# A hybrid decoder layer on one core: every PSUM tensor cut to 512 columns

## The chip, the core and the metric

The kernel runs on one core of one Trainium2 chip. The metric is the device time of one execution in microseconds; a kernel is timed in several runs and the median is compared. Matrix products run on TensorE (PE in the profile, its weight loads PEld), element-wise work on VectorE (DVE) and ScalarE (ACT). GpSimd (POOL) and SyncE (SP) issue the transfers. Products land in PSUM, which VectorE and ScalarE then read.

## What is computed

The layer normalises `x` (1024 tokens by 1024 channels), modulates it by a conditioning vector, projects it by one wide matrix, runs two gated linear recurrences in parallel, merges their projections and adds the result to `x`. Cut to what matters here:

```python
h = rms_norm(x, norm_w) * (1 + scale) + shift
proj = h @ w_in
hq, hf, hi, hz, gq, gk, gv, gz, ga, mg = split(proj)
y_h = hgrn2_branch(hq, hf, hi, hz, ...)   # 8 heads, 128 keys x 128 values each
y_g = gla_branch(gq, gk, gv, gz, ga, ...) # 4 heads, 128 keys x 256 values each
# both: S_t = diag(a_t) S_{t-1} + k_t v_t^T,  o_t = S_t^T q_t, per head
merged = sigmoid(mg0) * (y_h @ w_branch0) + sigmoid(mg1) * (y_g @ w_branch1)
out = rms_norm(x + gate * (merged @ w_out), final_norm_w)
```

## The kernel before, in words

Products are taken as float32r in three parts (high times high, high times low, low times high), each matmul 128 x 128 weights by 512 columns. The program goes through these stages.

- **First group** (`product`, L386): six feature blocks `f` of the projection, for the first and then for the second half of the tokens. Six accumulators of 512 columns are open at once: four are the halves of two 1024-column tiles `pd` (`accs`, L380 and the lines around it), two are the halves of the scoring tile `sc_ps`. `qk_out` reads each on VectorE (L362, L364) and sends it away.
- **V stages** (`Vstage`, `Vjob`, L1879): the values `gv`, and later `hi`, by a seven-product scheme (`PRODUCTS`), each product in two jobs `kk`. A stage has four banks `i` of 512 columns, again the halves of two `pd` tiles. After the second job of a product `Vstage.after` reads bank `i` (L1762, L1764 on ScalarE; L1786, L1790 on VectorE; for product 3 ScalarE writes a seed back, L1782). A job goes through `i` = 0, 1, 2, 3, six matmuls each.
- **Feature jobs** (`Feat`, `mm_feat`, L594): one head's gate, query or key feature for all 1024 tokens into one `pd` tile, both halves in turn; then one reader takes all 1024 columns: `silu_done` (L949 ScalarE, L950 VectorE), `gla_k_done` (L1016), `hf_done` (L1079, L1080 ScalarE).
- **Heads** (`attention`): side work that is woven between the matmuls of the jobs. VectorE builds `xb` (L645 to L648), TensorE makes the first level's scores in `sc_ps` (L652), VectorE reads them (L659 and the three predicated copies L664 to L666), TensorE makes the second level (L683) in the same tile, and so on.
- **Last stages** (L1330) **and the output product** (L1507): banks of 512 columns are lent by `Banks`: two halves of `sc_ps`, two `pm` tiles, four halves of two `pd` tiles.

PSUM holds eight banks of 512 float32 columns: `ps_d` two tiles of two banks, `sc_ps` one of two banks, `ps_m` two of one bank.

Up to the end of the first half of the first group the order on TensorE, ScalarE and VectorE is the order of the code. After it a scheduler sets the order on each engine from a priority and its own estimate of when operands are free, and it places the semaphore waits. It keeps track of a tile as a whole: a write to a tile is ordered after earlier reads of that tile, whichever columns they took. Each engine then runs its instructions strictly in that order. Slots in SBUF are given out in rotation, so a load can also wait for the last reader of its slot.

Of the kernel before, what the change touches and what calls it, by code (L numbers as in the profile page):

```python
# [16 lines left out]
P = 128  # L17
D = 1024
T = 1024
# [70 lines left out]
def hybrid_trunk_kernel(  # L90
# [20 lines left out]
    def dtile():  # L111
        cnt[0] += 1
        return ps_d.tile([P, T], F32, tag="d", name=f"pd{cnt[0]}")

# [3 lines left out]

    sc_ps = ps_s.tile([P, T], F32, name="sc_ps")

# [108 lines left out]
    def keep_busy(n):  # L229
        for _ in range(n):  # L230
            nc.tensor.matmul(sc_ps[:, 512:640], ones, ident, start=True, stop=True)

# [354 lines left out]
    def mm_feat(wt, rhs, ps, w=P):  # L587
        hi, lo = wt
        for k in range(KT):
            n = 0  # L590
            r_hi, r_lo = rhs(k)
            for a, b in ((hi, r_hi), (hi, r_lo), (lo, r_hi)):
                for th in range(2):
                    nc.tensor.matmul(ps[0:w, th * 512:(th + 1) * 512], a[:, k, 0:w],  # L594
                                     b[:, th * 512:(th + 1) * 512],
                                     start=(k == 0 and n == 0), stop=(k == KT - 1 and n == 2))
                n += 1
            yield
# [27 lines left out]
    def attention(q, k, f, v, V, post, early, lead=3):  # L626
# [23 lines left out]
        for b in range(32):  # L650
            ch, j = b // 4, b % 4
            nc.tensor.matmul(sc_ps[32 * j:32 * j + 32, ch * P:ch * P + 80], k[:, b * 32:b * 32 + 32], xb[:, b, :],  # L652
                             start=True, stop=True)
# [10 lines left out]
        cpr(bv[:, :, :, 1:4], bc(mk[:, :, :, 0:5:2], [NCH, 8, 3]), px[:, :, :, 0:5:2])  # L664
        cpr(bv[:, :, :, 2:4], bc(mk[:, :, :, 1:6:4], [NCH, 8, 2]), px[:, :, :, 1:6:4])
        cpr(bv[:, :, :, 3], bc(mk[:, :, :, 3], [NCH, 8]), px[:, :, :, 3])  # L666
        TT(k4[:, :, :, 0:3], k4[:, :, :, 0:3], f4[:, :, :, 1:4], M)
# [13 lines left out]
        for b in range(32):  # L681
            ch, j = b // 4, b % 4
            nc.tensor.matmul(sc_ps[32 * j:32 * j + 32, ch * 48:ch * 48 + 48], k[:, b * 32:b * 32 + 32],  # L683
                             xf[:, b * 48:b * 48 + 48], start=True, stop=True)
# [32 lines left out]
        keep(16)  # L717
        px = sc_ps[:, 0:384].rearrange("p (g s n) -> p g s n", s=6, n=4)
        bv = blk.rearrange("p c t -> p (c t)").rearrange("p (g r n) -> p g r n", r=4, n=4)
# [19 lines left out]
        for b in range(32):  # L739
            ch, j = b // 4, b % 4  # L740
            nc.tensor.matmul(sc_ps[32 * j:32 * j + 16, 512 + ch * 16:512 + ch * 16 + 16],
                             k16[:, b * 16:b * 16 + 16], q16[:, b * 16:b * 16 + 16], start=True, stop=True)
        for ch in range(NCH):
            for hf in range(2):
                i = 2 * ch + hf
                p0, c0 = 64 * hf + 32 * (ch % 2), ch // 2 * 32
                nc.tensor.matmul(sc_ps[p0:p0 + 32, c0:c0 + 32], k32[:, i * 32:i * 32 + 32],
                                 q32[:, i * 32:i * 32 + 32], start=True, stop=True)
        for ch in range(NCH):
            s0 = ch * P  # L750
            p0, c0 = ch % 2 * 64, 640 + ch // 2 * 64
            nc.tensor.matmul(sc_ps[p0:p0 + 64, c0:c0 + 64], k[:, s0:s0 + 64],
                             q[:, s0 + 64:s0 + 128], start=True, stop=True)
        grow(64)
        cur = off[1]
        cpr(blk[:, :, 16:32], bc(masks[16], [NCH, 16]),
            sc_ps[:, 512:640].rearrange("p (c t) -> p c t", c=NCH))
        for hf in range(2):
            for odd in range(2):
                p0 = 64 * hf + 32 * odd  # L760
                nc.scalar.copy(scT[64 * hf:64 * hf + 32, odd::2, 64 * hf + 32:64 * hf + 64],
                               sc_ps[p0:p0 + 32, 0:128].rearrange("p (c t) -> p c t", t=32))
        for odd in range(2):
            nc.scalar.copy(scT[0:64, odd::2, 64:128],
                           sc_ps[64 * odd:64 * odd + 64, 640:896].rearrange("p (c t) -> p c t", t=64))
        scoring.discard(me)
# [179 lines left out]
    def silu_done(store, key):  # L946
        def f(ps):
            s = S.get([T])
            nc.scalar.activation(s, ps, AF.Sigmoid)  # L949
            nc.vector.tensor_mul(s, s, ps)  # L950
            store[key] = s
        return f
# [60 lines left out]
    def gla_k_done(h):  # L1013
        def f(ps):
            t = S.get([T])
            nc.vector.tensor_copy(t, ps)  # L1016
# [59 lines left out]
    def hf_done(h):  # L1076
        def fn(ps):
            f, k = S.get([T]), S.get([T])
            nc.scalar.activation(f, ps, AF.Sigmoid)  # L1079
            nc.scalar.activation(k, ps, AF.Sigmoid, scale=-1.0)  # L1080
# [568 lines left out]
    def scores_done():  # L1649
        while scoring or head_no[0] < 12:  # L1650
            stream.weave(1)
        R.lend([sc_ps[:, 0:512], sc_ps[:, 512:1024]])

# [93 lines left out]
    class Vstage:  # L1747
# [226 lines left out]
```

## Time and profile before

| | |
|---|---|
| median of 3 runs | 1201.26 us (1200.64 to 1201.57) |
| the profiled execution: its own time | 1201.55 us |
| its span, first to last instruction | 1199.8 us |
| first group | 20 to 116 us |
| V stage of `gv` | 112 to 199 us |
| feature jobs and GLA heads, V stage of `hi` within | 199 to 423 us |
| feature jobs and HGRN heads | 423 to 797 us |
| last stages and output product | 797 to 1200 us |

A row of the timeline gives the start, the duration, engine, line, operation, `out<-in`, the size, the count of merged instructions and, in brackets, the time that the engine was idle before it and who ended that idle time. Matmuls are pipelined: one of 512 columns is shown 0.39 us long while the next starts 0.23 us after it, so a shown idle time understates a gap between starts by some 0.16 us.

### The profile page before, as it was taken

To read this page: it belongs to the slowest core of one execution; us is meant where nothing else is said; L and a number is where in the kernel's file an instruction comes from. 1 tells how busy PE (TensorE), PEld (TensorE's weight loads), DVE (VectorE), ACT (ScalarE), POOL (GpSimd) and SP (SyncE) were. 2 spreads that over 40 slices of the span, in tenths; PEclk is the share of its full clock that TensorE was granted. 3 is DMA by queue.
4 is the path that set the end of the run, shared out by engine and by line. 5 is a ranking of instruction groups with operands and counts; after the bars stand their busy time and mean duration, and the time that the engine had idled before them with its cause. 6 is when DMAs were issued, how large, how long until landed. Compare 5 with 4: busy or idle time off the path is not lost.

```text
span 1199.8 us, 20303 instructions
## 1 busy us (share of the span) xinstructions
PE 1170.1 (98%) x8137; PEld 951.0 (79%) x8137; DVE 846.3 (71%) x1270; ACT 584.9 (49%) x860; POOL 124.3 (10%) x257
## 2 busy tenths in 40 slices
PE   7999999999999999999999999999999999999997
PEld 6776777888878688888888878778888888878886
DVE  4745667657664955887897798695553866988994
ACT  5674462673455445334433435456643644444554
POOL 4111111000110211111111010001120000000000
PEclk9999999999999999999999999999999999999999
DMA  9745445155474855665565454255688846335523
GB/s 324 262 173 201 150 161 176 52 178 175 167 273 141 296 195 161 209 210 160 173 197 178 130 203 124 78 169 179 225 312 284 285 152 210 125 108 173 171 99 134
DMA packets 150641, 221.24 MB, mean 184 GB/s; under 512 B 8971, under 2 KB 107329, under 8 KB 150546
## 3 DMA queue, kind: packets, MB, share of 16 engines
q1 hardware_dynamic: 132114, 158.37, 42.4%
q0 software_dynamic: 18384, 61.56, 13.3%
q8 instruction: 64, 1.05, 0.4%
q14 instruction: 31, 0.25, 0.1%
q10 hardware_dynamic: 48, 0.01, 0.0%
HBM read 154.37 MB, written 65.54 MB: 183 GB/s over the span
## 4 chain that ended last, share of the span: by engine, by line
PE 65%; issue 20%; DVE 6%; ACT 4%; DMA 3%; POOL 2%; SPq 0%; POOLq 0%; DVEq 0%; ACTq 0%
PE pd L594 16%; PE pd L1330 11%; PE pd L1879 9%; PE sc_ps L1330 6%; PE pm L1330 6%; PE pd L1507 3%; PE pd L386 2%; PE sc_ps L1507 2%; PE pm L1507 1%; PE pm L798 1%; POOL ws L1182 1%; DVE b L212 1%; PE pm L817 1%; DMA b<-in_ada_w_dram 1%; PE sc_ps L386 1%
## 5 line engine op out<-in xcount | busy, mean ns | idle before, releaser
L594 PE MATMUL pd<-b,b 128*128 128x512 f32 x1632 | 393.8, 396 | 0.2 <-ACT b L1762 0.2
L594 PEld LDWEIGHTS pd<-b,b 128*128 128x128 f32 x1632 | 303.0, 189 | 65.8 <-issue 0.7
L1330 PE MATMUL pd<-b,b 128*128 128x512 f32 x720 | 173.2, 392 | 0.6 <-DVE b L1422 0.4
L1879 PE MATMUL pd<-b,b 128*128 128x512 f32 x672 | 162.7, 396 | 7.1 <-DVE b L1790 3.4
L1330 PEld LDWEIGHTS pd<-b,b 128*128 128x128 f32 x720 | 133.9, 188 | 31.2 <-DVE b L1422 0.9
L1879 PEld LDWEIGHTS pd<-b,b 128*128 128x128 f32 x672 | 123.4, 188 | 40.7 <-ACT b L1762 4.0
L212 DVE TENSOR_TENSOR b<-b,b 128x1024 fp32r<-128x1024 f32 x78 | 94.2, 1222 | 48.4 <-ACT b L211 48.1
L1273 DVE TENSOR_TENSOR b<-b,b 128x1024 fp32r<-128x1024 f32 x56 | 68.2, 1221 | 69.2 <-ACT b L1272 53.0
L1272 ACT CAST b<-b 128x1024 fp32r<-128x1024 f32 x56 | 58.4, 1050 | 65.0 <-PE pm L1330 18.1
L211 ACT CAST b<-b 128x1024 fp32r<-128x1024 f32 x78 | 79.8, 1047 | 6.4 <-PE pd L1879 3.0
L1330 PE MATMUL sc_ps<-b,b 128*128 128x512 f32 x324 | 78.7, 391 | 0.4 <-ACT b L1302 0.4
L1330 PE MATMUL pm<-b,b 128*128 128x512 f32 x300 | 72.1, 389 | 0.0
L1330 PEld LDWEIGHTS sc_ps<-b,b 128*128 128x128 f32 x324 | 60.4, 188 | 13.9 <-ACT b L1302 1.1
L1249 ACT CAST b<-b 128x1024 fp32r<-128x1024 f32 x48 | 49.7, 1050 | 43.9 <-PE pd L1330 15.9
L1250 DVE TENSOR_TENSOR b<-b,b 128x1024 fp32r<-128x1024 f32 x48 | 57.7, 1219 | 18.4 <-ACT b L1249 12.2
L1330 PEld LDWEIGHTS pm<-b,b 128*128 128x128 f32 x300 | 56.3, 188 | 11.7
L203 DVE TENSOR_TENSOR b<-b,b 128x1024 fp32r<-128x1024 f32 (+1 forms) x36 | 35.1, 983 | 29.5 <-ACT b L202 29.4
L386 PE MATMUL pd<-b,b 128*128 128x512 f32 x192 | 52.3, 405 | 2.8 <-DVE b L362 1.9
L1182 POOL DMA_DIRECT2D ws<-b x64 | 34.9, 546 | 193.6 <-DVE b L1174 107.4
L703 ACT COPY xb<-b 128x512 f32<-128x512 f32 x48 | 29.7, 621 | 50.8 <-PE sc_ps L683 23.8
L817 PE MATMUL pm<-scT,b 128*128 128x128 f32 x256 | 46.9, 275 | 0.0
L386 PEld LDWEIGHTS pd<-b,b 128*128 128x128 f32 x192 | 34.4, 188 | 15.4 <-DVE b L362 2.9
(317 smaller groups left out, 1699.6 us busy)
## 6 DMA issues: line engine op xcount, KB each, us to landing
b<-in_w_in_dram SPq DMA_DIRECT2D x72, 512.0 KB, 4.3
ws<-b POOLq DMA_DIRECT2D x64, 256.0 KB, 3.9
b<-ws SPq DMA_DIRECT2D x32, 512.0 KB, 4.4
b<-in_x_dram SPq DMA_DIRECT2D x16, 512.0 KB, 4.4
b<-in_ada_w_dram SPq DMA_DIRECT2D x32, 256.0 KB, 6.5
v<-b POOLq DMA_DIRECT2D x32, 256.0 KB, 3.7
b<-v SPq DMA_DIRECT2D x16, 512.0 KB, 5.2
b<-fx SPq DMA_DIRECT2D x16, 512.0 KB, 4.5
```

The lines of the kernel that those rows point to most:

```text
L211: held(nc.scalar.copy(hi, src))
L212: nc.vector.tensor_sub(lo, src, hi.bitcast(F32))
L386: nc.tensor.matmul(accs[f], wg(a, d, f), b[d][:, half * 512:half * 512 + 512], start=(d == 0 and n == 0), stop=(d == KT - 1 and n == 2))
L594: nc.tensor.matmul(ps[0:w, th * 512:(th + 1) * 512], a[:, k, 0:w], b[:, th * 512:(th + 1) * 512], start=(k == 0 and n == 0), stop=(k == KT ...
L817: nc.tensor.matmul(o, vch(ch)[:, vh * P:(vh + 1) * P], scT[:, ch, :], start=True, stop=(ch == 0))
L1249: nc.scalar.copy(hi, src)
L1250: nc.vector.tensor_sub(lo, src, hi.bitcast(F32))
L1272: nc.scalar.copy(hi, t)
L1273: nc.vector.tensor_sub(lo, t, hi.bitcast(F32))
L1330: nc.tensor.matmul(o, a[:, sl], c, start=(p in (1, 5) and kt == 0 and n == 0), stop=(kt == 3 and n == 2), skip_group_check=True)
L1507: nc.tensor.matmul(o, a, b, start=(p in (1, 5) and kt == 0 and n == 0), stop=(kt == 3 and n == 2), skip_group_check=True)
L1879: nc.tensor.matmul(st.bank[i], x_, w_, start=(p in (1, 5) and kk == 0 and a == 0 and n == 0), stop=(kk == 1 and a == 1 and n == 2), skip_g ...
```

## The change

`ps_d` now has four tiles of one bank each instead of two of two. `dtile` returns a list of two of them, and the scoring tile is a list of two. All users take the halves from these lists. The order of the code is kept; where one instruction read 1024 columns of PSUM there are now two of 512: the reads of the feature jobs, and those of the first level's scores (one product with the identity mask and three predicated copies per half). Every other PSUM access is of the same size as before. Lines below L653 have moved by up to six.

```diff
-    ps_d = ctx.enter_context(tc.tile_pool(name="ps_d", bufs=2, space=bass.MemoryType.PSUM))
+    ps_d = ctx.enter_context(tc.tile_pool(name="ps_d", bufs=4, space=bass.MemoryType.PSUM))
...
     def dtile():
         cnt[0] += 1
-        return ps_d.tile([P, T], F32, tag="d", name=f"pd{cnt[0]}")
+        return [ps_d.tile([P, 512], F32, tag="d", name=f"pd{cnt[0]}_{i}") for i in range(2)]
...
-    sc_ps = ps_s.tile([P, T], F32, name="sc_ps")
+    sc_ps = [ps_s.tile([P, 512], F32, name=f"sc_ps{i}") for i in range(2)]
...
-    acc0 = [dtile(), dtile()]
-    accs = [acc0[f // 2][:, (f % 2) * 512:(f % 2) * 512 + 512] for f in range(4)]
-    accs += [sc_ps[:, 0:512], sc_ps[:, 512:1024]]
+    accs = dtile() + dtile()
+    accs += sc_ps
...
-                    nc.tensor.matmul(ps[0:w, th * 512:(th + 1) * 512], a[:, k, 0:w],
+                    nc.tensor.matmul(ps[th][0:w, :], a[:, k, 0:w],
...
-        pc = sc_ps.rearrange("p (c t) -> p c t", t=P)
-        TT(blk, pc[:, :, 0:32], bc(eye32.unsqueeze(1), [NCH, 32]), M)
-        px = pc[:, :, 32:80].rearrange("p c (g s) -> p c g s", s=6)
-        bv = blk.rearrange("p c (g r) -> p c g r", r=4)
         mk = masks[1][:, :, :, 0].unsqueeze(1)
         cpr = nc.vector.copy_predicated
-        cpr(bv[:, :, :, 1:4], bc(mk[:, :, :, 0:5:2], [NCH, 8, 3]), px[:, :, :, 0:5:2])
-        cpr(bv[:, :, :, 2:4], bc(mk[:, :, :, 1:6:4], [NCH, 8, 2]), px[:, :, :, 1:6:4])
-        cpr(bv[:, :, :, 3], bc(mk[:, :, :, 3], [NCH, 8]), px[:, :, :, 3])
+        for z in range(2):
+            pc = sc_ps[z].rearrange("p (c t) -> p c t", t=P)
+            bz = blk[:, 4 * z:4 * z + 4]
+            TT(bz, pc[:, :, 0:32], bc(eye32.unsqueeze(1), [4, 32]), M)
+            px = pc[:, :, 32:80].rearrange("p c (g s) -> p c g s", s=6)
+            bv = bz.rearrange("p c (g r) -> p c g r", r=4)
+            cpr(bv[:, :, :, 1:4], bc(mk[:, :, :, 0:5:2], [4, 8, 3]), px[:, :, :, 0:5:2])
+            cpr(bv[:, :, :, 2:4], bc(mk[:, :, :, 1:6:4], [4, 8, 2]), px[:, :, :, 1:6:4])
+            cpr(bv[:, :, :, 3], bc(mk[:, :, :, 3], [4, 8]), px[:, :, :, 3])
...
             s = S.get([T])
-            nc.scalar.activation(s, ps, AF.Sigmoid)
-            nc.vector.tensor_mul(s, s, ps)
+            for th in range(2):
+                sl = slice(th * 512, th * 512 + 512)
+                nc.scalar.activation(s[:, sl], ps[th], AF.Sigmoid)
+                nc.vector.tensor_mul(s[:, sl], s[:, sl], ps[th])
...
-            pair = [dtile() for _ in range(2)]
-            self.bank = [pair[i // 2][:, i % 2 * 512:i % 2 * 512 + 512] for i in range(4)]
+            self.bank = dtile() + dtile()
...
     lent = [dtile() for _ in range(2)]
-    R.lend([pd[:, i * 512:i * 512 + 512] for pd in lent[::-1] for i in range(2)])
+    R.lend([pd for pds in lent[::-1] for pd in pds])
```

The order of the instructions moves with it. TensorE at the end of the first group, where the V stage begins; `pd_173` and `pd_174` hold the blocks `f` = 0, 1 and 2, 3, `sc_ps` 4 and 5, `pd_1137` and `pd_1138` are the V stage's two pairs of banks. The first of each run of matmuls stands here. Before:

```order
L386 MATMUL pd_173<-b_146,b_162 128x512
L386 MATMUL pd_174<-b_146,b_162 128x512
L386 MATMUL sc_ps<-b_146,b_168 128x512
L386 MATMUL pd_173<-b_146,b_162 128x512 [waits DVE_49]
L386 MATMUL sc_ps<-b_146,b_168 128x512 [waits DVE_49]
L1879 MATMUL pd_1137<-b_1076,b_139 128x512 [waits DVE_49,Activation_49]
L386 MATMUL pd_174<-b_146,b_162 128x512 [waits DVE_49]
L1879 MATMUL pd_1138<-b_1076,b_139 128x512 [waits DVE_49]
```

And of the changed kernel, where each block has a tile of its own:

```order
L385 MATMUL pd_0_174<-b_147,b_163 128x512
L385 MATMUL pd_1_175<-b_147,b_163 128x512
L385 MATMUL pd_0_176<-b_147,b_163 128x512
L385 MATMUL pd_1_177<-b_147,b_163 128x512
L385 MATMUL sc_ps_72<-b_147,b_169 128x512
L385 MATMUL sc_ps_73<-b_147,b_169 128x512
L1884 MATMUL pd_0_1140<-b_1079,b_140 128x512 [waits DVE_49,Activation_49]
L1884 MATMUL pd_1_1141<-b_1079,b_140 128x512 [waits DVE_49]
L1884 MATMUL pd_0_1142<-b_1079,b_140 128x512 [waits DVE_49]
L1884 MATMUL pd_1_1143<-b_1079,b_140 128x512 [waits DVE_49]
```

Before, the second block of each pair waits for VectorE (the read of the first), and the blocks are taken in the order 0, 2, 4, 1, 5, 3 with V matmuls ahead of block 3. Now blocks 0 to 5 follow each other without a wait, and the four banks of the V stage each wait once for VectorE.

TensorE in the V stage of `gv`, from the second job of product 7 to product 4's first job (`b_1499` and after it `b_1504` are the weights of the former, `b_1541` and `b_1546` of the latter). Before:

```order
L1879 MATMUL pd_1137<-b_1499,b_1505 128x512 [waits Activation_49]
L1879 MATMUL pd_1138<-b_1499,b_1505 128x512
L1879 MATMUL pd_1137<-b_1499,b_1505 128x512 [waits DVE_49]
L1879 MATMUL pd_1137<-b_1541,b_1545 128x512 [waits DVE_49,Activation_49]
L1879 MATMUL pd_1138<-b_1499,b_1505 128x512 [waits DVE_49]
```

Now:

```order
L1884 MATMUL pd_0_1140<-b_1504,b_1510 128x512 [waits Activation_49]
L1884 MATMUL pd_1_1141<-b_1504,b_1510 128x512
L1884 MATMUL pd_0_1142<-b_1504,b_1510 128x512
L1884 MATMUL pd_1_1143<-b_1504,b_1510 128x512
L1884 MATMUL pd_0_1140<-b_1546,b_1550 128x512 [waits DVE_49,Activation_49]
L1884 MATMUL pd_1_1141<-b_1546,b_1550 128x512 [waits DVE_49]
```

Before, banks 1 and 3 of product 7 wait for VectorE within the job. Now all four banks run on, and the wait for VectorE stands at the same bank's next use, one job later.

VectorE at the first level's scores of the first head. Before:

```order
L659 TENSOR_TENSOR blk<-sc_ps,eye_712 128x256 [waits PE_49,Pool_49]
L667 TENSOR_TENSOR b_1521<-b_1521,b_863 128x256x3 [waits DMAHW0_49,DMASW5_49]
L664 COPY_PREDICATED blk<-mask_716,sc_ps 128x64x3 [waits DVE_49,Pool_49]
L679 TENSOR_TENSOR xb<-xb,tot_758 128x64x4
L665 COPY_PREDICATED blk<-mask_716,sc_ps 128x64x2 [waits DVE_49]
L685 TENSOR_TENSOR b_1519<-xb,tot_758 128x64x12 [waits DVE_49,Activation_49]
L666 COPY_PREDICATED blk<-mask_716,sc_ps 128x64 [waits DVE_49]
```

Now:

```order
L662 TENSOR_TENSOR blk<-sc_ps_72,eye_715 128x128 [waits PE_49,Pool_49]
L679 TENSOR_TENSOR xb<-b_1524,tot_761 128x128x4 [waits DVE_49,PE_49]
L665 COPY_PREDICATED blk<-mask_719,sc_ps_72 128x32x3 [waits DVE_49,Pool_49]
L662 TENSOR_TENSOR blk<-sc_ps_73,eye_715 128x128 [waits PE_49]
L666 COPY_PREDICATED blk<-mask_719,sc_ps_72 128x32x2 [waits DVE_49]
L665 COPY_PREDICATED blk<-mask_719,sc_ps_73 128x32x3 [waits DVE_49]
L667 COPY_PREDICATED blk<-mask_719,sc_ps_72 128x32 [waits DVE_49]
L666 COPY_PREDICATED blk<-mask_719,sc_ps_73 128x32x2 [waits DVE_49]
L668 TENSOR_TENSOR b_1526<-b_1526,b_866 128x256x3 [waits DMAHW0_49,DMASW5_49]
L667 COPY_PREDICATED blk<-mask_719,sc_ps_73 128x32 [waits DVE_49]
L680 TENSOR_TENSOR xb<-xb,tot_761 128x64x4
```

Four reads have become eight of half the size, the two halves' reads alternate, and the last step of the second level's input (`xb`, L679 before, L680 now) stands behind all of them.

More of the change, by code (lines that the diff above doesn't have):

```diff
@@ L230, in keep_busy @@
         for _ in range(n):
-            nc.tensor.matmul(sc_ps[:, 512:640], ones, ident, start=True, stop=True)
+            nc.tensor.matmul(sc_ps[1][:, 0:128], ones, ident, start=True, stop=True)
     def turn_x(half, xs, d):
@@ L651, in attention @@
             ch, j = b // 4, b % 4
-            nc.tensor.matmul(sc_ps[32 * j:32 * j + 32, ch * P:ch * P + 80], k[:, b * 32:b * 32 + 32], xb[:, b, :],
+            nc.tensor.matmul(sc_ps[ch // 4][32 * j:32 * j + 32, ch % 4 * P:ch % 4 * P + 80], k[:, b * 32:b * 32 + 32], xb[:, b, :],
                              start=True, stop=True)
@@ L682, in attention @@
             ch, j = b // 4, b % 4
-            nc.tensor.matmul(sc_ps[32 * j:32 * j + 32, ch * 48:ch * 48 + 48], k[:, b * 32:b * 32 + 32],
+            nc.tensor.matmul(sc_ps[0][32 * j:32 * j + 32, ch * 48:ch * 48 + 48], k[:, b * 32:b * 32 + 32],
                              xf[:, b * 48:b * 48 + 48], start=True, stop=True)
@@ L740, in attention @@
             ch, j = b // 4, b % 4
-            nc.tensor.matmul(sc_ps[32 * j:32 * j + 16, 512 + ch * 16:512 + ch * 16 + 16],
+            nc.tensor.matmul(sc_ps[1][32 * j:32 * j + 16, ch * 16:ch * 16 + 16],
                              k16[:, b * 16:b * 16 + 16], q16[:, b * 16:b * 16 + 16], start=True, stop=True)
@@ L746, in attention @@
                 p0, c0 = 64 * hf + 32 * (ch % 2), ch // 2 * 32
[L747 removed]
+                nc.tensor.matmul(sc_ps[0][p0:p0 + 32, c0:c0 + 32], k32[:, i * 32:i * 32 + 32],
                                  q32[:, i * 32:i * 32 + 32], start=True, stop=True)
@@ L750, in attention @@
             s0 = ch * P
-            p0, c0 = ch % 2 * 64, 640 + ch // 2 * 64
-            nc.tensor.matmul(sc_ps[p0:p0 + 64, c0:c0 + 64], k[:, s0:s0 + 64],
+            p0, c0 = ch % 2 * 64, 128 + ch // 2 * 64
+            nc.tensor.matmul(sc_ps[1][p0:p0 + 64, c0:c0 + 64], k[:, s0:s0 + 64],
                              q[:, s0 + 64:s0 + 128], start=True, stop=True)
@@ L1015, in f @@
             t = S.get([T])
-            nc.vector.tensor_copy(t, ps)
+            for th in range(2):
+                nc.vector.tensor_copy(t[:, th * 512:th * 512 + 512], ps[th])
             if h == 3:
@@ L1651, in scores_done @@
             stream.weave(1)
-        R.lend([sc_ps[:, 0:512], sc_ps[:, 512:1024]])
+        R.lend(sc_ps)
     def side_done():
```

14 lines of the change are left out of this document (8 added, 6 removed).

## The prediction

> **What bounds the kernel now.** I read the page first, then the chain of waits, then TensorE's idle times in the timeline.
>
> ```profile
> span 1199.8 us, 20303 instructions
> PE 1170.1 (98%) x8137; PEld 951.0 (79%) x8137; DVE 846.3 (71%) x1270; ACT 584.9 (49%) x860; POOL 124.3 (10%) x257
> ...
> PE 65%; issue 20%; DVE 6%; ACT 4%; DMA 3%; POOL 2%; SPq 0%; POOLq 0%; DVEq 0%; ACTq 0%
> ```
>
> TensorE is shown busy for 98% of the span, so only its stops can be won: the change removes no matmul and adds none. How long a matmul really takes is read from an undisturbed piece of the chain of waits (start, duration, what):
>
> ```profile
> 1179.62 5.44 PE pd L1507 x24
> ```
>
> 24 matmuls of 512 columns in 5.44 us are 0.2267 us each. In the middle of the HGRN heads nothing is to be won; five head periods (a stretch with its engines' busy times):
>
> ```profile
> 450.46:664.36 213.90, 213.90 (x2002) 178.68 (x2002) 167.93 (x297) 86.98 (x134) 32.70 (x60) 1.00 0.58 183
> ```
>
> TensorE (first) has no idle time in 213.90 us, and VectorE (third) is busy for 167.93, or 33.6 of a period's 42.8. The stops lie in the first group's end, the two V stages and at a few places later, and there the releaser is mostly a read of PSUM. So the end is set by TensorE's stream, and a stop removed is worth its time as long as the operands behind it are ready.
>
> **The change part by part.** A read of one half of a pair of banks no longer holds back a matmul into the other half.
>
> *A. End of the first group.* Matmuls of L386, of L1879, then rows of the timeline:
>
> ```profile
> 105.77:116.39 10.62, 4.81 (x19) 1.00 0.28 105
> ...
> 105.77:116.39 10.62, 3.41 (x14) 1.00 0.28 105
> ```
>
> ```profile
> 109.15 0.68 DVE L362 TENSOR_SCALAR b<-pd 128x512 f32<-128x512 f32 x1
> 109.89 0.96 PE L386 MATMUL pd<-b,b 128*128 128x512 f32 x3 [1.92 <-DVE b L362]
> 112.16 1.23 DVE L212 TENSOR_TENSOR b<-b,b 128x1024 fp32r<-128x1024 f32 x1 [0.58 <-ACT b L211]
> 116.39 6.96 PE L1879 MATMUL pd<-b,b 128*128 128x512 f32 x29 [0.32 <-DVE b L362]
> ```
>
> 19 and 14 are 33, two of which only touch the edges: 31 matmuls, worth 31 x 0.2267 = 7.03 us, took 10.62, so 3.59 are lost. Block 1 waited 1.92 us for the read of block 0, in the other half of its tile, and that read stood late in VectorE's line. Now the 18 matmuls of blocks 0 to 5 run on and end at 105.77 + 4.08 = 109.85, when the first read is ending (109.83), so V bank 0 starts at once. What is late next is bank 2: it starts 12 matmuls later, at 112.6, and VectorE, in its new order, has by then to read blocks 0, 1, 4, 5 and 2 and do one L212, 5 x 0.68 + 1.23 = 4.6 us from 109.15, so to 113.8 at most. A wait of up to 1.2 us is left: **2.4 us** won at least and 3.6 at most; I take 2.5.
>
> *B. V stage of `gv`.*
>
> ```profile
> 116.39:199.11 82.72, 76.73 (x323) 1.00 0.50 173
> ```
>
> ```profile
> 123.58 11.29 PE L1879 MATMUL pd<-b,b 128*128 128x512 f32 x48 [0.22 <-ACT b L1764]
> 135.09 11.26 PE L1879 MATMUL pd<-b,b 128*128 128x512 f32 x48 [0.22 <-ACT b L1762]
> 146.57 21.22 PE L1879 MATMUL pd<-b,b 128*128 128x512 f32 x90 [0.23 <-ACT b L1762]
> 168.09 10.95 PE L1879 MATMUL pd<-b,b 128*128 128x512 f32 x47 [0.29 <-DVE b L1786]
> 177.57 2.36 DVE L212 TENSOR_TENSOR b<-b,b 128x1024 fp32r<-128x1024 f32 x2 [1.97 <-ACT b L211]
> 179.85 0.68 DVE L1790 TENSOR_TENSOR b<-pd,b 128x512 f32<-128x512 f32 x1
> 180.59 1.89 PE L1879 MATMUL pd<-b,b 128*128 128x512 f32 x7 [1.55 <-DVE b L1790]
> 183.65 5.69 PE L1879 MATMUL pd<-b,b 128*128 128x512 f32 x24 [1.17 <-DVE b L1790]
> 197.04 1.67 PE L1879 MATMUL pd<-b,b 128*128 128x512 f32 x6 [0.18 <-ACT b L1762]
> ```
>
> The 240 matmuls from 123.58 to 183.65 (48 + 48 + 90 + 47 + 7) took 60.07 us against 54.41, a loss of 5.66; a stop shown as 0.22 costs about 0.6 from start to start (135.09 - 123.58 - 48 x 0.2267 = 0.63). With the stop at 116.39 to 123.58 (7.19 - 29 x 0.2267 = 0.62) and the one at 197.04 (0.6) that is 6.9. Every releaser is the read of a bank. The two largest stops are the pattern shown in the order: bank 1 of product 7 waited for L1790, which stood behind two L212. Now bank 0 is wanted again only after 18 more matmuls (4.1 us): the last matmul of bank 0 came some 1.1 us before the stop, at 177.6, so the next use is at 181.7, and L1790 ended at 180.5. The cover is 1.2 us; if VectorE falls behind by more, the stop comes back one job later. Loads move with TensorE, since they wait for slots that this work frees. The full 6.9 asks that no operand be late after a gain of 9 us; I take **5.5**, bounds 2.5 (only the small stops, 4 x 0.6) and 6.9.
>
> *C. V stage of `hi`.*
>
> ```profile
> 359.14 3.04 PE L1879 MATMUL pd<-b,b 128*128 128x512 f32 x12 [0.65 <-ACT b L1762]
> 399.85 0.88 PE L1879 MATMUL pd<-b,b 128*128 128x512 f32 x2 [0.61 <-ACT b L211]
> 401.36 2.56 PE L1879 MATMUL pd<-b,b 128*128 128x512 f32 x10 [0.64 <-DVE b L212]
> 404.57 4.60 PE L1879 MATMUL pd<-b,b 128*128 128x512 f32 x19 [0.65 <-DVE b L1790]
> 418.04 0.89 PE L683 MATMUL sc_ps<-xb,b 128*32 128x48 f32 x64 [0.61 <-DVE xb L679]
> 420.73 0.96 PE L594 MATMUL pd<-b,b 128*128 128x512 f32 x3 [0.22 <-ACT b L1762]
> ```
>
> With 0.38 added to each shown idle time (0.6 against 0.22) these are 1.0 each, and 0.6 the last. The waits for L211, L212 and L679 are for operands and stay. The one for L1790 goes, but the wait for L679, behind it in VectorE's line, will take its 1.0. 359.14 and 420.73 go: 1.6, and scoring groups that had been cut in two are whole again, some 0.4. I take **2.0** (0.6 to 3.0).
>
> *D. Later places.*
>
> ```profile
> 801.57 0.59 PE L683 MATMUL sc_ps<-xb,b 128*32 128x48 f32 x34 [1.29 <-DVE blk L666]
> 834.35 3.00 PE L1330 MATMUL sc_ps<-b,b 128*128 128x512 f32 x12 [0.42 <-ACT b L1302]
> 1064.24 1.20 PE L1330 MATMUL pd<-b,b 128*128 128x512 f32 x4 [0.44 <-DVE b L1422]
> ```
>
> 1.7, 0.8 and 0.8 by the same addition. The last two are one bank held by a read of its neighbour. At 801.57 the second level writes only the first half now, but its input stands behind all eight reads; part of the wait stays. I take **2.0** (0.8 to 3.3).
>
> *E. What is added.* Reads in halves, and eight small reads for four per head.
>
> ```profile
> L950 DVE TENSOR_TENSOR b<-b,pd 128x1024 f32<-128x1024 f32 x24 | 29.8, 1241 | 20.7 <-ACT b L949 20.6
> L1790 DVE TENSOR_TENSOR b<-pd,b 128x512 f32<-128x512 f32 x8 | 5.3, 682 | 0.1
> L664 DVE COPY_PREDICATED blk<-mask,sc_ps 128x192 f32<-128x192 int32 x12 | 5.3, 441 | 0.0
> L725 DVE COPY_PREDICATED blk<-mask,sc_ps 128x64 f32<-128x64 int32 x24 | 5.3, 223 | 0.0
> ```
>
> Two halves of a feature's read cost 2 x 682 - 1241 = 123 ns more on VectorE. A half-size predicated copy is in no row: at most as long as a whole one (0.44, so 4 x 0.44 = 1.8 us a head), at least as the small one of L725 (0.22, so nothing); I take 0.9. With three feature reads that is about 1.2 us of VectorE in a period that leaves it 42.8 - 33.6 = 9.2 free. So it lies beside the matmuls, and its price is **0**; without that cover it would be 1.2 a head. [...]
>
> **Sum**: 2.5 + 5.5 + 2.0 + 2.0 = 12.0 us. The profiled execution took 1201.55 us (1.75 around its span), 0.29 above the median: 1201.26 - 12.0 = 1189.3. All lower bounds give 2.4 + 2.5 + 0.6 + 0.8 = 6.3 won, 1195.0; all upper ones 3.6 + 6.9 + 3.0 + 3.3 = 16.8, 1184.5.
>
> **The rivals.**
>
> *VectorE and ScalarE take over.* From 159 to 183 us the chain of waits ran through them and a load (5.57 us for `qk`), not through TensorE. If that chain is no shorter, the stops in A and B come back as waits for operands, and only the small ones stay won: 1.2 + 4 x 0.6 + 1.4 in C and D = 5, 1196.3. For it: VectorE's line is full from 177 on. Against it: the chain starts from a read of a finished bank, so it moves with TensorE.
>
> *Slower: the added reads make VectorE late for scoring.* It happened once before, with another cause:
>
> ```profile
> 704.64 1.31 PE L652 MATMUL sc_ps<-xb,b 128*32 128x80 f32 x64 [1.89 <-DVE xb L648]
> ...
> 704.60:709.40 4.80, 4.76 (x73) 3.88 (x74) 4.80 (x8) 1.62 (x3) 0.00 (x0) 0.65 0.79 265
> ```
>
> The stop cost 1.89 + 0.38, and the granted clock then fell to 0.65 for 4.8 us, another 1.7: 4.0 in all. It decides from four heads on (16 against the 12 won); with five, 1189.3 + 20 = 1209. Against it: the free 9.2 us of a period, some eight times the addition. [...]
>
> *More than forecast: the stop at 704.64 goes too*, its line on VectorE being earlier: 1189.3 - 4.0 = 1185.3. Nothing in the order there favours it.
>
> *No effect*: the scheduler's order already filled the waits, and the same stops come back at other names: 1201. Against it: the waits within a job are gone from the order.
>
> **How the numbers follow.** The forecast has 0.61, VectorE taking over 0.19, more than forecast 0.06, no effect 0.08, slower 0.06. Within 0.2% (2.4 us, about what a measurement of this kernel can tell from no change) is only the no-effect case; faster holds 0.61 + 0.19 + 0.06 = 0.86. The range reaches from all upper bounds (1184.5) to a little above the first rival (1197.5); the last two cases, 0.14, are left out.
>
> **What would show it.** Right: no idle time at L385 with releaser L362 near 108 us; V matmuls (L1884) from 110 to 190 us with a loss below 2 us; no idle time with releasers L1767, L1769, L1791 or L1795 in the V stages; period of the HGRN heads still 42.8 us. Wrong: new idle times with releasers L211 or L212, or with the load of `qk`, of the same size (first rival); idle time ahead of L652 or its like in several heads, with the clock below 1.00 (second). If VectorE's reads of halves take longer than 0.44 us each, E was wrong.

## The result, and the profile after

The changed kernel takes 1182.03 us (median of 4 runs, 1179.97 to 1182.65) against 1200.95 of the kernel before on the same chip (1199.9 to 1201.57): a ratio of 0.984 with a 95% interval of 0.9824 to 0.9855. So 18.9 us were won where 12.0 were forecast; the time lies 2.5 us below the range.

The first lines and the chain's shares of the page of the changed kernel:

```profile
span 1181.0 us, 20415 instructions
...
PE 1159.9 (98%) x8137; PEld 953.5 (81%) x8137; DVE 848.3 (72%) x1344; ACT 587.8 (50%) x900; POOL 123.9 (10%) x257
...
PE 61%; issue 24%; DVE 5%; DMA 4%; ACT 3%; POOL 3%; SPq 1%; POOLq 0%; ACTq 0%; DVEq 0%
```

TensorE's busy time fell by 10.2 us (1170.1 to 1159.9) though it runs the same 8137 matmuls. Matmuls are pipelined: in the changed kernel one of L593 is shown 0.395 us long on average, while the 24 from 1076.24 us on start 0.2267 us apart. So a stop that is shown as short, or not at all, still counts as busy time (one of 1.91 us from start to start, at 387 us, is shown as 1.52). That is why stops were measured from start to start.

To see where the time went, both traces are cut at the same matmul, counted by its line (the 24th of the V stage, the first of the features, and so on). The stretches of the kernel before, then of the changed one (start:end, length, busy time and instructions of PE, PEld, DVE, ACT, POOL, granted clock, DMA share, GB/s):

```profile
118.80:199.11 80.31, 76.44 (x443) 59.44 (x441) 56.20 (x66) 36.12 (x48) 11.89 (x22) 1.00 0.49 170
...
662.40:797.39 134.99, 132.36 (x1311) 108.97 (x1310) 111.06 (x188) 60.53 (x95) 7.60 (x14) 0.99 0.44 138
797.39:1116.49 319.10, 316.79 (x1576) 259.47 (x1574) 222.19 (x253) 160.32 (x210) 17.23 (x32) 1.00 0.61 203
319.69:452.84 133.15, 129.54 (x1052) 104.77 (x1051) 87.94 (x146) 67.96 (x103) 19.46 (x36) 1.00 0.68 230
```

```profile
116.09:189.41 73.32, 73.32 (x442) 60.38 (x440) 56.92 (x72) 36.34 (x49) 11.86 (x22) 1.00 0.52 183
...
651.28:783.21 131.93, 130.60 (x1312) 107.92 (x1311) 111.18 (x207) 61.65 (x108) 7.57 (x14) 1.00 0.44 141
783.21:1097.77 314.56, 314.31 (x1575) 260.50 (x1574) 220.80 (x257) 158.59 (x210) 17.15 (x32) 1.00 0.62 205
310.60:441.71 131.11, 128.53 (x1052) 106.60 (x1051) 88.51 (x156) 68.21 (x104) 19.38 (x36) 0.99 0.70 233
...
439.33:653.23 213.90, 213.90 (x2002) 178.69 (x2002) 168.42 (x327) 88.42 (x155) 32.73 (x60) 1.00 0.58 183
```

Each kernel was profiled three times in all (below). With the lengths of all six profiles:

| stretch (first matmul to first matmul) | before, three profiles | after, three profiles | won (means) | forecast |
|---|---|---|---|---|
| first group, to the 24th V matmul (A) | 97.62, 97.63, 97.63 | 95.73, 95.75, 95.82 | 1.9 | 2.5 |
| V stage of `gv` (B) | 80.30, 80.50, 80.60 | 73.32, 73.32, 73.32 | 7.1 | 5.5 |
| features and GLA heads | 120.59, 121.49, 121.41 | 121.18, 121.03, 121.16 | 0.0 | 0 |
| V stage of `hi` (C) | 133.15, 133.17, 133.07 | 131.11, 129.22, 133.23 | 1.9 | 2.0 |
| five HGRN heads (E) | 209.56, 209.56, 209.40 | 209.57, 209.43, 209.47 | 0.0 | 0 |
| last three HGRN heads | 134.99, 133.99, 134.14 | 131.93, 131.41, 131.42 | 2.8 | 0 |
| last stages, to their last matmul (D) | 319.09, 319.17, 320.35 | 314.57, 314.07, 314.03 | 5.3 | 2.0 |

The start of the first group varies from profile to profile (19.8 to 23.0 us over all kernels) and is left out; the sum is 19.0 without it. Two rows carry most of the miss: D, and the last three heads.

The mean of C hides a large spread. The same stretch of the changed kernel in its second and its third profile:

```profile
310.07:439.29 129.22, 126.97 (x1053) 105.39 (x1051) 88.23 (x156) 68.23 (x104) 19.38 (x36) 1.00 0.70 237
```

```profile
310.78:444.01 133.23, 129.50 (x1052) 107.17 (x1051) 88.57 (x156) 68.20 (x104) 19.37 (x36) 0.97 0.69 230
```

The granted clock (third figure from the end) is 1.00 in the one, 0.97 in the other and 0.99 in the first profile.

### The profile page after: what moved, and what is told of

Read it like the earlier page. It is cut to its first block, busy times and chain, and to the rows that moved or that the text cites. A ratio compares the mean times of both kernels' runs of the same rounds, so it can differ in the third digit from the quotient of the medians.

```text
span 1181.0 us, 20415 instructions
## 1 busy us (share of the span) xinstructions
PE 1159.9 (98%) x8137; PEld 953.5 (81%) x8137; DVE 848.3 (72%) x1344; ACT 587.8 (50%) x900; POOL 123.9 (10%) x257
## 4 chain that ended last, share of the span: by engine, by line
PE 61%; issue 24%; DVE 5%; DMA 4%; ACT 3%; POOL 3%; SPq 1%; POOLq 0%; ACTq 0%; DVEq 0%
PE pd L593 15%; PE pd L1884 11%; PE pd L1336 9%; PE sc_ps L1336 5%; PE pm L1336 4%; PE pd L1513 3%; PE pd L385 2%; PE sc_ps L1513 2%; PE pm L1513 1%; POOL ws L1188 1%; PE pm L799 1%; DMA b<-in_ada_w_dram 1%; PE pm L818 1%; PE sc_ps L385 1%; PE pm L820 1%
## 5 line engine op out<-in xcount | busy, mean ns | idle before, releaser
L593 PE MATMUL pd<-b,b 128*128 128x512 f32 x1632 | 391.9, 395 | 0.2 <-DVE b L212 0.2
L593 PEld LDWEIGHTS pd<-b,b 128*128 128x128 f32 x1632 | 302.1, 188 | 65.1 <-issue 0.7
L1336 PE MATMUL pd<-b,b 128*128 128x512 f32 x720 | 169.7, 390 | 0.2 <-ACT pd L1319 0.2
L1884 PE MATMUL pd<-b,b 128*128 128x512 f32 x672 | 159.0, 395 | 3.5 <-ACT b L211 1.5
L1336 PEld LDWEIGHTS pd<-b,b 128*128 128x128 f32 x720 | 134.8, 188 | 28.7 <-ACT pd L1319 0.7
L212 DVE TENSOR_TENSOR b<-b,b 128x1024 fp32r<-128x1024 f32 x78 | 94.3, 1222 | 36.0 <-ACT b L211 35.7
L211 ACT CAST b<-b 128x1024 fp32r<-128x1024 f32 x78 | 79.8, 1047 | 12.4 <-DMA v<-b 4.2
L1336 PE MATMUL sc_ps<-b,b 128*128 128x512 f32 x324 | 77.2, 390 | 0.0
L1336 PE MATMUL pm<-b,b 128*128 128x512 f32 x300 | 71.1, 389 | 0.0
L1336 PEld LDWEIGHTS sc_ps<-b,b 128*128 128x128 f32 x324 | 60.8, 188 | 12.6
L1336 PEld LDWEIGHTS pm<-b,b 128*128 128x128 f32 x300 | 56.3, 188 | 11.7
L385 PE MATMUL pd<-b,b 128*128 128x512 f32 x192 | 51.7, 404 | 0.9 <-ACT b L202 0.8
```

The costliest lines, as they stand in the source:

```text
L211: held(nc.scalar.copy(hi, src))
L212: nc.vector.tensor_sub(lo, src, hi.bitcast(F32))
L385: nc.tensor.matmul(accs[f], wg(a, d, f), b[d][:, half * 512:half * 512 + 512], start=(d == 0 and n == 0), stop=(d == KT - 1 and n == 2))
L593: nc.tensor.matmul(ps[th][0:w, :], a[:, k, 0:w], b[:, th * 512:(th + 1) * 512], start=(k == 0 and n == 0), stop=(k == KT - 1 and n == 2))
L1336: nc.tensor.matmul(o, a[:, sl], c, start=(p in (1, 5) and kt == 0 and n == 0), stop=(kt == 3 and n == 2), skip_group_check=True)
L1884: nc.tensor.matmul(st.bank[i], x_, w_, start=(p in (1, 5) and kk == 0 and a == 0 and n == 0), stop=(kk == 1 and a == 1 and n == 2), skip_g ...
```

## Experiments: which part does what

**Accumulators alone.** The four accumulating banks are tensors of their own; the scores stay as before.

```diff
-        return ps_d.tile([P, T], F32, tag="d", name=f"pd{cnt[0]}")
+        return [ps_d.tile([P, 512], F32, tag="d", name=f"pd{cnt[0]}_{i}") for i in range(2)]
...
+    accs = dtile() + dtile()
+    accs += [sc_ps[:, 0:512], sc_ps[:, 512:1024]]
```

> Only the four accumulating banks are made four tensors of 512 columns (the features' reads are then in halves by necessity); the scores' tensor stays one of 1024 and its first-level reads stay whole. Theory (the tie between the two halves of an accumulating pair is what held TensorE in the first group and the two V stages): the first group and the V stage of gv give about 8.9 us as in the full change, the V stage of hi about 1, the stop at 801.57 (1.5 us with its restart) stays, so about 1201 - 10.5 = 1190.5 us, and the stop at 704.64 stays if it has to do with the scores' reads. Rival (the gain needs the scores' tensor divided too, since the first group accumulates in it as well): under 5 us won, 1196 or more.

Measured: 1187.68 us (ratio 0.9896, 0.9881 to 0.9912), 2.8 below what the first theory said. By stretches, in the table's order: 96.38, 73.44, 121.76, 129.53, 209.67, 133.51, 314.77. So B, C and most of D (4.8 of 5.3) come from the accumulators. Two rows fall short of the full change: A by 0.6, as block 5 now waits for the read of block 4 in the scores' tensor (1.3 us shown), and the last three heads by 1.9. Against the expectation the stop at 801.57 went too, though the scores' tensor was whole:

```profile
787.06 4.24 PE L1334 MATMUL pd<-b,b 128*128 128x512 f32 x18
791.24 0.89 PE L682 MATMUL sc_ps<-xb,b 128*32 128x48 f32 x64
```

18 matmuls of the last stages now stand ahead of the second level, where the kernel before had 12.

**Scores alone.** Only `sc_ps` is divided, with the reads in halves that go with it.

```diff
-    sc_ps = ps_s.tile([P, T], F32, name="sc_ps")
+    sc_ps = [ps_s.tile([P, 512], F32, name=f"sc_ps{i}") for i in range(2)]
```

> Only the scores' tensor is made two of 512 columns, with the first-level reads in halves; the accumulating pairs stay whole. Theory: the stop at 801.57 goes (1.5 us), scoring groups cut in two in the V stage of hi become whole (about 0.5), the rest stays: 1201 - 2 = 1199 us. Rival (the parts only pay together, or the stop at 704.64 goes by the earlier score reads): 704.64 gives 3 to 4 us more, 1195.5 us.

Measured: 1197.31 us (0.9971, 0.996 to 0.9982). Stretches: 97.59, 80.08, 120.92, 132.97, 209.56, 131.99, 317.25. Against the means of the kernel before, 2.4 us come from the last three heads and 2.3 from D: halfway between the two theories. By the medians the two parts won 14.0 and 4.3 alone, 18.3 as a sum, against 18.9 for both. Stretch by stretch they do not simply add: in D 4.8 and 2.3 alone are 5.3 together, in the last three heads 0.9 and 2.4 are 2.8.

**Reads in halves alone.** Whole tensors as before, the reads as in the changed kernel.

```diff
+        for z in range(2):
+            pc = sc_ps[:, z * 512:z * 512 + 512].rearrange("p (c t) -> p c t", t=P)
...
+                nc.scalar.activation(s[:, sl], ps[:, sl], AF.Sigmoid)
+                nc.vector.tensor_mul(s[:, sl], s[:, sl], ps[:, sl])
```

> All tensors stay as before; only the reads are made in halves (features, first-level scores), so the price of the added instructions stands alone. Theory (they lie beside TensorE's matmuls): 1201 us within 1 us, head period still 42.78 us, VectorE busy for about 1.0 us more per head. Rival (the halves lengthen VectorE's line ahead of scoring): each head period longer by 0.3 us or more, 1204 us or more.

Measured: 1206.14 us (1.0043, 1.0029 to 1.0058): slower, against the first theory. TensorE's waits (line, releaser, us in total, times, longest), of the kernel before and then of this one:

```profile
PE sc_ps L683 <- DVE blk L666: 1.3, 1, 1.3
```

```profile
PE sc_ps L685 <- DVE blk L668: 4.3, 5, 2.4
```

The second level, which writes the same tensor, waits for the last first-level read five times instead of once. That is 3.0 us more, as much as this profiled execution (1204.53 us) was slower than that of the kernel before. The free 9.2 us of a head period did not cover this: what counts is how far the last read stands from the matmul that it holds, not how much of the period VectorE is idle.

**Twice as many reads on divided tensors.** The changed kernel with the first-level reads in quarters.

```diff
-        for z in range(2):
-            pc = sc_ps[z].rearrange("p (c t) -> p c t", t=P)
+        for z in range(4):
+            pc = sc_ps[z // 2][:, z % 2 * 256:z % 2 * 256 + 256].rearrange("p (c t) -> p c t", t=P)
```

> The changed kernel with the first-level reads of the scores in quarters, 16 reads a head where it has 8: VectorE gets about 1 us more a head. Theory (with the scores in two tensors the second level waits for the first half's reads alone, so the free time of a head period covers it): 1182 us, head period 42.78. Rival (the line of VectorE ahead of the second level counts, not the free time of the period, as where the reads were halved on whole tensors): stops of 0.3 to 1 us ahead of the second level in most of the 8 HGRN heads, 1185 to 1188 us.

Measured: 1181.7 us (0.9832, 0.9818 to 0.9846), as without (1181.54 on the same chip). A half-size predicated copy of the changed kernel, and a quarter here:

```profile
L665 DVE COPY_PREDICATED blk<-mask,sc_ps 128x96 f32<-128x96 int32 x24 | 7.1, 296 | 0.0
```

```profile
L665 DVE COPY_PREDICATED blk<-mask,sc_ps 128x48 f32<-128x48 int32 x48 | 10.9, 228 | 0.0
```

So price 0 holds in the changed kernel even for twice the additions, and fails on whole tensors: the second level writes only the first tensor now and needs only that one's reads done.

## Experiments: the stop ahead of the sixth HGRN head's scoring

In this head VectorE also sums eight rows of the gate's weights (`gate_side`). The first load's wait on VectorE and the scoring's wait on TensorE, before and after:

```profile
689.48 0.75 DVE L1051 TENSOR_SCALAR b<-b,cs 128x1024 f32<-128x1024 f32 x1 [1.62 <-DMA b<-in_ada_w_dram]
```

```profile
677.27 0.75 DVE L1055 TENSOR_SCALAR b<-b,cs 128x1024 f32<-128x1024 f32 x1 [0.54 <-DMA b<-in_ada_w_dram]
...
692.53 1.31 PE L651 MATMUL sc_ps<-xb,b 128*32 128x80 f32 x64 [0.91 <-DVE xb L647]
```

From start to start the stop was 2.28 us with a wait of 1.62, and 1.30 with one of 0.54. Five kernels and four more profiles followed.

*Each load one step ahead*, on the kernel before (`rows.append(gate_row(k + 1))` ahead of the sum of row `k`):

> The kernel before, with each row of the gate's weights loaded one step ahead of the VectorE instruction that uses it (loads, arithmetic and PSUM layout unchanged). Theory (the stop at 704.64 comes from VectorE standing 1.6 us before the first of these loads, and the granted clock falls behind it): no idle time ahead of the first-level scoring of that head and no stretch with a clock below 1.00 there, 3.7 to 4.0 us won, 1197.2 us. Rival (VectorE's line is late for another reason, the load only happens to end last): the stop keeps 1 us or more and the time is within 1.5 us of 1201.

Measured: 1201.77 us (1.0001, 0.9992 to 1.0009). The edit did not reach its aim: the scheduler put the first sum where it had been, and the wait stayed, so the run decides nothing.

```profile
689.58 0.75 DVE L1059 TENSOR_SCALAR b<-b,cs 128x1024 f32<-128x1024 f32 x1 [1.28 <-DMA b<-in_ada_w_dram]
```

*The sums on GpSimd*, on both kernels:

```diff
-                nc.vector.scalar_tensor_tensor(gacc, b, cs[:, k:k + 1], gacc, ALU.mult, ALU.add)
+                nc.gpsimd.tensor_scalar_mul(b, b, cs[:, k:k + 1])
+                nc.gpsimd.tensor_add(gacc, gacc, b)
```

> The kernel before, with the eight rows of the gate's weights multiplied and summed on GpSimd (two instructions a row) and no longer on VectorE, so that VectorE waits for none of these loads; all else as before. Theory (that wait makes the stop at 704.64): scoring of that head starts without a stop, 1.96 us won, and 1.6 more where the granted clock fell behind it: 1198 us, between 1197.4 and 1199.3. Rival (VectorE's line is too full there in any case): a stop of 0.7 us or more stays, 1200 us or more.

> The changed kernel with the same sums on GpSimd. Theory: the stop of 0.98 us goes, and those of 0.2 to 0.3 us near 708 and 759, 1180.7 us. If the stop is already as small by chance in most executions: 1182 us. Rival (GpSimd's sums hold its DMA issues back, and stores come later): 1183 us or more.

Measured: 1223.36 us (1.0183, 1.0166 to 1.0199) and 1205.1 us (1.0024, 1.0013 to 1.0035): 22 to 24 us lost on either, for a cause that no theory held. Rows of the timeline of the first:

```profile
704.64 3.20 POOL L1054 TENSOR_TENSOR b<-b,b 128x1024 f32<-128x1024 f32 x1
...
705.56 2.77 DVE L648 TENSOR_TENSOR xb<-xb,b 128x256 f32<-128x256 f32 x1
```

VectorE's L648 took 0.63 us in the kernel before; here it takes 2.77 and ends 0.49 after GpSimd's sum. So this too says nothing about the load.

*The sums kept in program order*, which puts them behind the scoring, on both kernels:

```diff
+        rows = [gate_row(0)]
+        yield 3
...
+                held(nc.vector.tensor_scalar_mul(gacc, b, cs[:, 0:1]))
```

> The kernel before, with the gate's sums kept in program order on VectorE and their first load three steps ahead, so that they stand behind the sixth HGRN head's scoring and VectorE waits for no load ahead of it. Theory: the stop of 1.96 us ahead of that scoring goes, with 1.6 us of lower clock in the executions that have it: 1198.5 us (1197.8 to 1199.5). Rival (the time of the sums only moves to another head's scoring): a stop of 0.7 us or more ahead of another scoring group, 1200.5 us or more.

> The changed kernel with the same move. Theory: the stop of 0.8 to 1.4 us ahead of that scoring goes: 1181.8 - 1.1 = 1180.7 us. Together with the same move on the kernel before it tells how much of the full change's gain lies in that stop: the difference of the two should be about 1198.5 - 1180.7 = 17.8 us, against 19.7 without the move. Rival (as above): 1181.5 us or more.

Measured: 1198.13 us (0.9962, 0.995 to 0.9975) and 1179.59 us (0.9823, 0.9803 to 0.9843). The stop is gone in both, and the stretch of the last three heads is now nearly as long in the one as in the other:

```profile
664.16:794.32 130.16, 129.75 (x1312) 108.08 (x1310) 111.76 (x188) 61.05 (x96) 7.73 (x14) 1.00 0.44 143
```

```profile
656.33:785.86 129.53, 129.53 (x1312) 108.05 (x1310) 112.19 (x207) 61.62 (x108) 8.04 (x14) 1.00 0.44 143
```

0.6 us are left of the 2.8 that the change wins there, so most of that gain hangs on this head's sums and their loads. Without that head the change is worth 0.9962 - 0.9823 = 1.4% or 16.7 us by the ratios, 18.5 by the medians. That the last kernel is faster than the changed one is not shown: the intervals overlap.

*More profiles*, since a wait for a load could be chance:

> The kernel before, a second profile. Theory (the wait for the first gate load is set by where the loads stand in the queue and what else is in flight, so it is a property of the kernel): VectorE waits 1.3 to 1.7 us for that load, the stop ahead of the scoring is 2.0 to 2.4 us from start to start. Rival (chance from execution to execution): a wait anywhere between 0.3 and 1.7 us. The fall of the granted clock at that place: there again if it belongs to the stop, elsewhere or absent if it is chance.

> The kernel before, a third profile; as for the second. Time lost between the 1200th and the last of the features' matmuls: 135.0 us between them with the fall of the clock, about 133.2 without.

> The changed kernel once more, for a second profile beside the runs of this chip. Theory (the stop ahead of the first-level scoring of the sixth HGRN head is VectorE's wait for the first gate load plus 0.7 us, and that load's landing differs by about a microsecond from execution to execution): 1182 us, the stop again the sum of that wait and 0.7 us, but not 1.0 us as before; the fall of the granted clock behind the stop at 387 us may be there or not. Rival (both are fixed by the order of the instructions): the stop 0.9 to 1.1 us again and the clock falls at the same place.

> The changed kernel, a third profile. Theory (property of the kernel): wait for the first gate load 0.3 to 0.6 us as in its two profiles so far, 131.2 to 131.9 us between the same two matmuls. Rival (chance): between 0.3 and 1.7 us.

In this order the times were 1201.76 and 1202.15 us (one execution each), 1181.54 (median of 4; ratio 0.9831, 0.9814 to 0.9848) and 1183.82 (one). One row of each kernel:

```profile
690.43 0.76 DVE L1051 TENSOR_SCALAR b<-b,cs 128x1024 f32<-128x1024 f32 x1 [1.44 <-DMA b<-in_ada_w_dram]
```

```profile
674.49 0.75 DVE L1055 TENSOR_SCALAR b<-b,cs 128x1024 f32<-128x1024 f32 x1 [0.35 <-DMA b<-in_ada_w_dram]
```

The waits are 1.62, 1.44, 1.53 before and 0.54, 0.35, 0.37 after; the stops, from start to start, 2.28, 2.12, 2.20 and 1.30, 1.13, 1.16: always the wait plus 0.7 to 0.8. So the shorter wait belongs to the change, not to chance. VectorE comes to this load at the same point in all six profiles, 27.9 to 28.0 us after the fifth head's scoring, so its line is neither earlier nor later. The load is issued at the same place too (23.2 to 23.4 us after that scoring) and used 6.1 to 6.4 us later before, 5.0 to 5.1 after: it lands sooner. With the scores alone divided the wait was 0.34, with the accumulators alone 1.26. In the changed kernel with reads in quarters it was 1.00. Why it lands sooner is not settled.

## Experiment: what is left of the V stage of `hi`

ScalarE and TensorE there in the changed kernel:

```profile
381.10 1.05 ACT L643 COPY xb<-b 128x1024 f32<-128x1024 f32 x1 [2.58 <-DMA b<-qk]
...
387.01 4.83 ACT L211 CAST b<-b 128x1024 fp32r<-128x1024 f32 x5
...
389.04 0.81 PE L1884 MATMUL pd<-b,b 128*128 128x512 f32 x2 [1.52 <-ACT b L211]
...
390.49 5.73 PE L1884 MATMUL pd<-b,b 128*128 128x512 f32 x17 [0.64 <-DVE b L212]
```

The casts for the next V job stand behind a copy that waits for the load of `qk`, two table loads (1.28 us each) and the inverse root. In its third profile the load came later:

```profile
382.79 1.06 ACT L643 COPY xb<-b 128x1024 f32<-128x1024 f32 x1 [4.16 <-DMA b<-qk]
...
390.73 1.22 PE L1884 MATMUL pd<-b,b 128*128 128x512 f32 x2 [3.10 <-ACT b L211]
```

Two more kernels moved the root of the third GLA head four steps later, so that casts come first, and the second also has the gate's sums in program order:

```diff
-            yield from inverse_root(rst, sq[0], 256)
+            yield from inverse_root(rst, sq[0], 256, 6 if h == 2 else 2)
```

> The changed kernel with the inverse root of the third GLA head four steps later, so that ScalarE makes five casts for the V jobs of hi ahead of the two table loads and the root, and no longer behind them. Theory (what is left of the V stage of hi is those casts' lateness, 1.5 + 0.9 us of stops at 387 to 390 us and 1.6 us more where the granted clock falls behind them): no waits of TensorE for L211 or L212 there, 1181.8 - 2.4 = 1179.4 us, 1178 with the fall. Rival (the casts wait for their slots, which the matmuls free, so the order on ScalarE does not matter): 1181 to 1182 us.

> The changed kernel with both moves, the later root and the gate's sums behind the scoring. Theory (they lie at two places and add): 1181.8 - 2.4 - 1.1 = 1178.3 us. Rival (what is won at 390 us moves later work onto loads that are late): 1180 us or more.

Measured: 1184.26 us (0.9849, 0.9836 to 0.9862) and 1182.88 (0.9842, 0.9827 to 0.9858): nothing won. The stop at the casts went and another came, ahead of the fourth GLA head's scoring:

```profile
403.84 0.89 PE L651 MATMUL sc_ps<-xb,b 128*32 128x80 f32 x39 [2.77 <-DVE xb L647]
```

VectorE's rows there:

```profile
395.12 0.42 DVE L1002 TENSOR_TENSOR b<-b,b 128x256 f32<-128x256 f32 x1 [2.40 <-ACT b L967]
...
403.15 0.63 DVE L647 TENSOR_TENSOR xb<-xb,b 128x256 f32<-128x256 f32 x1
```

VectorE stood 2.40 us for the root (L967). Its eight L1002, which need it, then came between reads of banks and casts without a break, and L646 and L647, which the scoring needs, stood behind them. The wait moved from ScalarE's line to VectorE's, and a smaller stop (1.2 us lost) came ahead of the first HGRN head's scoring. Neither theory held this.

## Why the prediction was right, and where it was wrong

**The bound and the mechanism were right; the sum was not.** The stream of matmuls sets the time, and stops at a neighbour's read went. No releaser of the list (L1767, L1769, L1791, L1795) is left among TensorE's waits in the V stages; five head periods still take 213.90 us.

**A** was forecast at 2.5 and gave 1.9, below its lower bound of 2.4. Block 1's wait went as said; the wait for bank 2 cost 1.5 us from start to start, over its allowance of 1.2. The 4.6 us of VectorE's work held every instruction, but not the 0.78 us that VectorE stood for a cast ahead of its L212:

```profile
109.15 3.00 PE L1884 MATMUL pd<-b,b 128*128 128x512 f32 x12
...
110.38 1.22 DVE L212 TENSOR_TENSOR b<-b,b 128x1024 fp32r<-128x1024 f32 x1 [0.78 <-ACT b L211]
111.53 1.28 DVE L364 COPY b<-sc_ps 128x512 f32<-128x512 f32 x2
...
112.72 1.28 DVE L362 TENSOR_SCALAR b<-pd 128x512 f32<-128x512 f32 x2
...
113.46 6.88 PE L1884 MATMUL pd<-b,b 128*128 128x512 f32 x29 [1.31 <-DVE b L362]
```

**B** was forecast at 5.5 (2.5 to 6.9) and gave 7.1, just over the upper bound. In the stretch of 73.32 us TensorE has no idle time at all. The doubt that operands would be late did not come true here, and the cover of 1.2 us for L1790 held.

**C** was forecast at 2.0 and gave 1.9 on average. That hit is luck, for it was 2.0, 3.9 and 0 in the three profiles. Where the granted clock held, 3.9 were won, more than the upper bound of 3.0. The wait for L679, which was to take over the 1.0 of L1790's, got shorter (0.61 us shown before, 0.40 after) and not longer. Gaps of under 0.2 us, many of them around scoring groups that are whole again, gave some 1.1 where 0.4 was reckoned. The waits for L211 and L212 stayed, as said, but the first of them grew from 0.61 us shown to 1.52, 1.22 and 3.10, as it hangs on the load of `qk`. In the first profile a fall of the granted clock behind it took another 1.6; in the third, with a mean of 0.97 over the stretch, the clock was at half for 6.8 us around it. The prediction had a term neither for that load nor for the clock here.

**D is the largest mis-sized term: 2.0 forecast (0.8 to 3.3), 5.3 measured.** Two things failed. First, "part of the wait stays" at 801.57: the order now puts 18 matmuls of L1336 ahead of the second level, where 12 came before it was cut in two, and nothing stays. It went with the accumulators alone too, so this order is enough; with the scores alone divided the 12 stayed and so did 0.27 us of the wait.

```profile
783.21 4.24 PE L1336 MATMUL pd<-b,b 128*128 128x512 f32 x18
787.38 0.89 PE L684 MATMUL sc_ps<-xb,b 128*32 128x48 f32 x64
788.19 9.81 PE L1336 MATMUL pd<-b,b 128*128 128x512 f32 x42
```

The three stops of the list gave 1.8, 0.7 and 0.7 with their restarts, about the upper bounds. Second, the sum had no term for gaps that are shown as no idle time. Late in these stages the kernel before changes banks after pieces of odd length, the changed one after whole products:

```profile
1097.41 2.43 PE L1330 MATMUL pm<-b,b 128*128 128x512 f32 x10
1099.77 3.02 PE L1330 MATMUL pd<-b,b 128*128 128x512 f32 x12
```

```profile
1076.24 5.60 PE L1336 MATMUL pd<-b,b 128*128 128x512 f32 x24
1081.68 5.60 PE L1336 MATMUL pm<-b,b 128*128 128x512 f32 x24
```

10 matmuls take 2.36 us there against 2.27, 24 take 5.44, exactly 24 x 0.2267. In the last 344 matmuls of these stages, which gave 1.7 us, the kernel before has nine such gaps of 0.04 to 0.11 us, 0.7 in all, beside the stop at 1064.24; the changed one has none. That the odd pieces make them is read from the two orders and not tested. The rest of D, some 1.4, is spread over small stops, among them one of 1.0 us in the third profile of the kernel before alone. The order of the instructions, from which the prediction argued elsewhere, could have shown the whole products.

**The last three heads are the term that was missing: 0 forecast, 2.8 measured.** The rival "more than forecast" named the right place with a chance of 0.06, because "nothing in the order there favours it". The failed step: the stop was taken to shrink only if VectorE's line came earlier, and the load that VectorE stands for in that line had no term. The line did not come earlier. The head's first gate load is there some 1.2 us sooner after its issue, in every profile of the two kernels, and the stop shrinks by 1.0; a third-level stop (1.15 to 0.3) and one at the state product (0.6) go with it, by the trace. That rival's price of 4.0 was not met either: the stop shrank and did not go, and the fall of the granted clock behind it, counted as 1.7, was in one of three profiles of the kernel before, where it cost 0.9, since a later stop of 1.15 then vanished.

**E** was right in the changed kernel: the period did not grow, and reads in quarters cost nothing that the time shows. The reason given, the 9.2 free microseconds, was wrong, as the reads on whole tensors show. A half-size predicated copy takes 0.30 us, within the bounds of 0.22 and 0.44.

The rivals: VectorE and ScalarE taking over was true only for C. Something like the slower one happened where the reads were halved without dividing the tensors, some 4.5 us. There TensorE waited ahead of the second level and not of the first scoring, and the clock did not fall behind the longest of these waits (2.4 us near 801 us, with 1.00 from 799 to 806); dividing the scores' tensor is what keeps this away.

## What to carry to other kernels

Where a dependency is tracked by tile, a tile of two banks makes the banks wait for each other; dividing it won the stops here (18.9 us by the medians) and also let the scheduler keep products whole, so gaps that no idle time shows, here of 0.04 to 0.11 us, belong in the sum. Do not weigh added reads against an engine's idle share: ask which matmul stands behind the last of them. A head that carries extra work and a load is its own case; read its line from the load on.

## What the runs showed of the hardware

**The granted clock fell behind some stops only.** In the changed kernel, around the stops of 1.91 and 1.11 us (start to start) at 387 and 389 us, then behind them:

```profile
387.13:390.49 3.36, 1.19 (x5) 0.38 (x3) 3.18 (x5) 3.36 (x4) 0.00 (x0) 1.00 0.42 121
390.49:394.05 3.56, 3.56 (x9) 2.81 (x10) 3.37 (x5) 2.39 (x3) 1.61 (x3) 0.53 1.00 287
```

Eight matmuls took 0.427 us each and not 0.227, 1.6 us lost; the clock was at 0.50 for 3.41 us. The same place showed no fall in the second profile (stops of 1.61 and 1.11, a clock of 1.00 over the stretch). In the kernel before, the stop of 2.12 to 2.28 at the sixth head was followed by a fall in one of three profiles: 0.50 for 3.41 us in the first; the second, with 1.00 over the stretch, is 1.0 us shorter, and the third 0.9. The stop of 2.31 at 107 us had none behind it in the first profile (1.00 from 106 to 118 us). One in the V stage of `gv`, shown as 1.55 us before 180.59, had none either (1.00 from 178 to 186 us); the same kernel with each load one step ahead stood there for 1.9 us, and the clock was 0.57, 0.50, 0.50 and 0.72 in the four microseconds from 180. What decides whether it falls is not shown.

**Beside GpSimd's sums two of VectorE's instructions took longer.** At the sixth head L648 took 0.63 us in the kernel before and 2.77 beside a GpSimd sum of 3.20, and ended 0.49 us after it; L656, next in line, took 0.64 there and 3.03 here, beside the next sum (2.36 us from 708.39). What holds them is not shown.
